# A hybrid decoder layer on one core: the GLU takes its columns by position in the chunk, and the last block's early u is computed from unscaled x

## The chip, the cores and the metric

The kernel runs on one core of one Trainium2 chip, as one program. The metric is the device time of one execution in microseconds (us). The engines are named as in the profile: PE is TensorE's matmul, PEld its weight load, DVE is VectorE, ACT is ScalarE, POOL is GpSimd, and SP is SyncE, which here issues most of the DMAs.

## The reference, cut to what matters

One decoder layer over 2064 tokens (16 meta tokens and 2048 others) of 1024 features, all in fp32:

```python
hn = rms_norm(h, norm_mix_g)                 # h * rsqrt(mean(h*h) + eps) * g
proj = hn @ w_in                             # columns: b_gate | c_gate | v | u, 512 each
conv_out = b_gate * causal_dwconv(c_gate * v, conv_w)       # width 3
y = s5(u)                                    # 32 groups, complex diagonal state, scan over tokens
g = gelu(y)
ssm_out = g * sigmoid(g @ w_glu)             # the GLU, 512 x 512
mixed = concat(rms_norm(conv_out), rms_norm(ssm_out))
h = h + mixed @ w_out
hn = rms_norm(h, norm_ffn_g)
up = causal_dwconv(hn @ w_up, ffn_conv_w, ffn_conv_b)       # 2 x 2816 columns
h = h + (silu(up[:2816]) * up[2816:]) @ w_down
y = rms_norm(h, norm_final_g)                # meta positions dropped
```

The 1/rms of a token is one number for all its features. So `proj` of a token can be computed from `x * g` without it, and be multiplied by it afterwards: `(x * g * rs) @ w = rs * ((x * g) @ w)`.

## The kernel before, in words

Features lie on the 128 partitions, tokens along the free dimension. The 2064 tokens are cut into six chunks of 344 columns (`QL`), numbered 0 to 5 (q), and three blocks of two chunks each (b = 0, 1, 2; 688 columns, `B2`). A chunk of x is loaded in two halves of four k-tiles (128 x 4 x 344, 688 KB).

**Every matmul is made of three.** Both operands are split into a high part (rounded to the matmul's fp32r format, a copy on ScalarE) and a low part (what is left, a subtraction on VectorE): `split_weights` (L122) for weights, `parts` (L246) for activations, which is the pair L248 and L109 in the profile. `product` (L128) issues high x high (L138), high weights x low activations (L139) and low weights x high activations (L142) for each k-tile, into one PSUM tile for both chunks of a block. With `by_chunk` all of chunk 0 comes first, then all of chunk 1; otherwise the chunks alternate by k-tile. Three PSUM tiles (`mm_tile`, L95) are in rotation.

**1/rms.** `inv_rms` (L173) squares the halves on ScalarE (L164, two buffers of tag `sq`), adds them on VectorE to one row of 344 columns (L109), sums over the partitions by matmuls with a column of ones (`st_...`, L188), takes the power -1/2 on GpSimd (L199), spreads the result on diagonals (`dg_...`, L203), broadcasts it to all partitions by a matmul (`sb_...`, L208), and copies it from PSUM on ScalarE (`rs_...`, L213).

**x in, two ways.** `raw_x` (L378) is used for chunks 0 and 1, at the kernel's start: it splits `x * g` at once, four k-tiles of a half by four short instructions on ScalarE (L389) and four on VectorE (L390), and computes 1/rms beside it, into the tile `rs0`; the products of block 0 are multiplied by it when they leave PSUM. `prep_x` (L348) is used for all others: it loads, computes 1/rms, scales x by g and 1/rms into a new tile (`t_c`, L241, eight short VectorE instructions for a chunk; tag `sq`), and splits that (L248, L109, one long instruction each for a half). With `late` the split is put off and emitted where `take_late` stands. The halves of x have three buffers (tag `xt`).

**Order of the work.** First u of block 0 (`u_block(0)`), then `conv_block(0)`, then u of block 2 (the "early u"), u of block 1, `conv_block(1)`, `conv_block(2)`. Beside block 0 the coefficients of the state space are computed, in memory (pool `a0`) that is given free when they are done; `start_a1` then opens the pools `xf2` (four split tiles) and `a1` in its place. There `prep_x(4, hu, other=True)` and `prep_x(5, hu, late=late)` are queued, chunks 4 and 5 for the early u: chunk 4's split goes to `xf2`, chunk 5's to the tiles that chunk 0 leaves after the last unit of `conv_block(0)`. The scan itself runs beside `conv_block(1)` and `conv_block(2)`. In the text the side work is made of generators, stepped after each unit; the framework then orders each engine's instructions with the text's order as priority and a model of durations, and inserts the waits. So an instruction can stand earlier on its engine than in the text, and an engine keeps the order that was set even where the chip's times are others.

`u_block` (L877) writes u from PSUM to `ut` in order of position in the chunk: token 8c + j goes to row j, column c. It does so on VectorE for block 0, where 1/rms is multiplied in (`mul`, L890), and on ScalarE otherwise (L892). The state space works on u in this order, and its result after gelu lies in DRAM (`g_d`) the same way.

**The GLU.** `load_glu` (L1012) brings the result into `gt`, 128 x 4 x 8 x 258: feature group, position j, column c. The matmuls want two-dimensional chunks of 344 columns. `tokens` (L1007) is a view of such a chunk that reads or writes it in the order of j, then c, with neighbours eight columns apart, so that the chunk itself is in token order. `prep_glu` (L1016) splits each chunk of `gt` through this view (`gh` on ScalarE, L1021; `gl` on VectorE, L109). `glu_block` (L1072) has four units of 24 matmuls for each chunk pair (`pg`), takes the sigmoid (`sg`, L1079) and multiplies `gt` by it in place, again through `tokens` (L1081). `prep_ssm` (L1026) norms and splits the result for the output projection, in token order (L1038, and `l_ms`, L1039), as x and the other half of the projection are in token order.

The tile for 1/rms of a whole block has one buffer (`rs_tile`, L373, tag `rsk`); after the projection it serves the MLP's norms (`prep_rs`, L1108). The MLP, from about 700 us to the end, is not touched.

Of the kernel before, what the change touches and what calls it, by code (L numbers as in the profile page):

```python
# [14 lines left out]
AF = mybir.ActivationFunctionType  # L15
ALU = mybir.AluOpType
# [6 lines left out]
NJ = 8  # L23
# [5 lines left out]
QL = 344  # L29
# [28 lines left out]
def layer_kernel(ctx, tc, xq, pk, w_in, w_glu, w_out, w_up, w_down, ssm_s, ssm_m, y):  # L58
    nc = tc.nc
    V, S, T, G = nc.vector, nc.scalar, nc.tensor, nc.gpsimd  # L60
# [7 lines left out]
    xf2 = None  # L68
# [33 lines left out]
    def f32(ap):  # L102
        return ap.bitcast(F32)

    def two(ap):
        return ap.rearrange("p (c t) -> p c t", c=2)

    def tt(out, a, b, op):
        V.tensor_tensor(out, a, b, op=op)  # L109

    def mul(out, a, b):
        tt(out, a, b, ALU.mult)
# [37 lines left out]
    def hl_tile(n, name, pool=None, tag="xhl", bufs=8):  # L150
        return (pool or xf).tile([P, 4, QM], F32R, tag=tag, bufs=bufs, name=name)[:, :, :n]
# [21 lines left out]
    def inv_rms(groups, n, name, out=None):  # L173


        s = sum_squares(groups, n, name)
        yield
        yield
        return (yield from inv_rms_of(s, 4 * P * len(groups), n, name, out))
# [193 lines left out]
    def rs_tile(name):  # L373
        return cp.tile([P, 2, QM], F32, tag="rsk", bufs=1, name=name)

    rs0 = rs_tile("rs0")[:, :, :QL]

    def raw_x(q, res):  # L378


        xs, out = [], []
        for i in range(2):
            xs += load_halves((xq[q, :, 4 * i : 4 * i + 4, :],), QL, f"c{q}{i}")
            yield
        for i, x in enumerate(xs):
            hi, lo = hl_tile(QL, f"h_c{q}_{i}"), hl_tile(QL, f"l_c{q}_{i}")
            for k in range(4):
                g = col(C_MIX + 4 * i + k)
                S.activation(hi[:, k, :], x[:, k, :], AF.Copy, scale=g)  # L389
                V.scalar_tensor_tensor(  # L390
                    out=lo[:, k, :], in0=x[:, k, :], scalar=g, in1=f32(hi[:, k, :]), op0=ALU.mult, op1=ALU.subtract
                )
            out.append((hi, lo))
            yield
        res.append(out)
        yield from inv_rms(xs, QL, f"c{q}", rs0[:, q, :])


    sgn = col(C_SGN)
# [456 lines left out]
    def after_unit(n=1, n_prep=1):  # L856
        if a1 is None:
            ssm.step(4)
            if not ssm.q:
                start_a1()  # L860
                prep.add(prep_x(4, hu, other=True), prep_x(5, hu, late=late))
        else:
            ssm.step(n)
            prep.step(n_prep)
# [12 lines left out]
    def u_block(b, hs, last=False):  # L877
        rhs = rhs_of(hs)
        for m in range(4):
            if last and m == 3:  # L880
                while len(late) < 2:
                    prep.step()
            ps = unit(rhs, f"pu_{b}_{m}", m == 0 or last and m == 3)
            ut = cvp.tile([P, NJ, 86], F32, tag="ut", bufs=2, name=f"ut_{b}_{m}")
            if last and m == 3:
                take_late(2)
            by_j = lambda a: a.rearrange("p c (x j) -> p c x j", j=NJ)
            out = ut.rearrange("p j (c x) -> p c x j", c=2)
            if b == 0:
                mul(out, by_j(ps[:, :, :QL]), by_j(rs0))  # L890
            else:
                S.activation(out, by_j(ps[:, :, :QL]), AF.Copy)  # L892
            dma(out=u_d[:, m, :, b * 86 : b * 86 + 86].rearrange("j p c -> p j c"), in_=ut)
            after_unit(n_prep=5 if last else 1)

    def conv_block(b, hs, late_after=False, n_prep=1):
        rhs = rhs_of(hs)

        for j in range(4):
            pv_ = unit(rhs, f"cv_{b}_{j}", False)  # L900
            vs = cvp.tile([P, B2], F32, tag="cs", bufs=3, name=f"vs_{b}_{j}")
            if b == 0:
                mul(two(vs), pv_[:, :, :QL], rs0)
            else:
                S.activation(two(vs), pv_[:, :, :QL], AF.Copy)
            after_unit(n_prep=n_prep)
            pc = unit(rhs, f"cc_{b}_{j}", False)
            cv = cvp.tile([P, B2 + 2], F32, tag="cvt", bufs=1, name=f"cvt_{b}_{j}")
            V.tensor_copy(cv[:, 0:2], halo[:, j, :])
            if b == 0:  # L910
                mul(two(vs), two(vs), rs0)
            tt(two(cv[:, 2:]), pc[:, :, :QL], two(vs), ALU.mult)
            V.tensor_copy(halo[:, j, :], cv[:, B2 : B2 + 2])
            tp = cvp.tile([P, B2], F32, tag="cs", bufs=3, name=f"tc_{b}_{j}")
            S.activation(tp, cv[:, 2:], AF.Copy, scale=col(C_CW + 8 + j))
            axpy(tp, cv[:, 1 : B2 + 1], col(C_CW + 4 + j), tp)
            axpy(tp, cv[:, 0:B2], col(C_CW + j), tp)
            if b == 0:
                mul(two(tp), two(tp), rs0)
            after_unit(n_prep=n_prep)  # L920
            if late_after and j == 3:
                while len(late) < 2:
                    prep.step()
            pb = unit(rhs, f"cb_{b}_{j}", j == 3)
            if late_after and j == 3:
                take_late(2)
            tt(two(tp), pb[:, :, :QL], two(tp), ALU.mult)
            dma(out=mx_d[2 * b : 2 * b + 2, :, j, :].rearrange("q p t -> p q t"), in_=two(tp))
            after_unit(n_prep=n_prep)
# [37 lines left out]

    hc = [[] for _ in range(3)]
    hu, late = [], []
    first = [raw_x(q, hc[0]) for q in range(2)]  # L970
    next(first[0])
    stream.raw.append(load_weights(*stream.items.popleft()))
    next(first[0])
# [5 lines left out]
    while first:  # L979
        for g in list(first):  # L980
            if next(g, prep) is prep:
                first.remove(g)
    u_block(0, hc[0])
    conv_block(0, hc[0], late_after=True, n_prep=4)

    prep.add(prep_x(2, hc[1]), prep_x(3, hc[1], other=True, late=late))
# [20 lines left out]
    def tokens(a):  # L1007

        names = "p k (c j) -> p k j c" if len(a.shape) == 3 else "p (c j) -> p j c"
        return a.rearrange(names, j=NJ)  # L1010
# [5 lines left out]
    def prep_glu(b, res, **kw):  # L1016
        for c in range(2):
            hi, lo = hl_tile(QL, f"gh_{b}_{c}", **kw), hl_tile(QL, f"gl_{b}_{c}", **kw)
            c0 = (2 * b + c) * 43
            src = gt[:, :, :, c0 : c0 + 43]  # L1020
            S.activation(tokens(hi), src, AF.Copy)  # L1021
            tt(tokens(lo), src, f32(tokens(hi)), ALU.subtract)
            res.append(((hi, lo),))
            yield

# [46 lines left out]
    def glu_block(b):  # L1072
        until(hg[b])
        rhs = rhs_of(hg[b])
        for m in range(4):
            ps = mm_tile(f"pg_{b}_{m}")
            product([ps[:, c, :QL] for c in range(2)], stream.take(), rhs, 4, by_chunk=m == 0)
            sg = ev_tile(f"sg_{b}_{m}")
            S.activation(two(sg), ps[:, :, :QL], AF.Sigmoid)  # L1079
            g = gt[:, m, :, b * 86 : b * 86 + 86]  # L1080
            mul(g, g, tokens(sg))  # L1081
            prep.step(2 if b else 1)

    hos = [[] for _ in range(3)]
# [587 lines left out]
```

## Time and profile before

| | |
|---|---|
| time, median of 3 runs | 2195.66 us (2195.51 to 2199.68) |
| the profiled execution's own time | 2199.4 us |
| its span, first to last instruction | 2197.6 us |
| granted TensorE clock, mean | 0.984 |
| busy DVE, share of the span | 77% |
| busy ACT, share of the span | 50% |

The profile is one execution. Each row of a group or of the order in time names the line, engine, operation, and `out<-in` by the program's tile names; durations are us unless marked ns; `[1.79 <-DVE sq_ms L109]` means that the engine stood idle for 1.79 us until VectorE finished writing `sq_ms`. A weight load (PEld) overlaps matmuls. The granted clock of a stretch is the mean share of TensorE's full clock. DMA-issuing instructions on SP show the time of the issue, not of the transfer.

### The profile page before, as it was taken

How to read it: one execution, taken by the hardware profiler on the slowest of the kernel's cores; microseconds unless marked ns; L12 is line 12 of the kernel's file. 1: busy time of each engine (PE TensorE's matmuls, PEld its weight loads, DVE VectorE, ACT ScalarE, POOL GpSimd, SP SyncE). 2: the span in 40 equal slices, each digit the busy share in tenths (PEclk: the TensorE clock that was granted, in tenths of full speed). 3: DMA queues.
4: the chain of work that ended last, by engine and by line, in shares of the span. 5: the costliest groups of instructions: out<-in, count | busy, mean ns of one | idle time of the engine just before them, and what ended most of it. 6: DMA issues, size and time to landing. Idle time of an engine off the chain costs nothing.

```text
span 2197.6 us, 33162 instructions
## 1 busy us (share of the span) xinstructions
PE 2119.1 (96%) x13012; PEld 2057.7 (94%) x13012; DVE 1688.0 (77%) x2539; ACT 1097.5 (50%) x1651; POOL 153.2 (7%) x174
## 2 busy tenths in 40 slices
PE   8997999999899999999999999999999999999997
PEld 7997999998898999999999999999899999999996
DVE  8896498857866796886679878777768878767776
ACT  4135333236523365554556556555456556545555
POOL 0000000000000001101110010100111010110010
PEclk9998999999999999999999999999999999999999
DMA  7376544352475336635552554744554362654463
GB/s 246 104 219 169 142 144 146 116 169 74 144 232 187 100 98 158 157 90 122 133 127 76 144 119 122 184 103 130 147 136 109 103 166 82 163 118 99 98 168 118
DMA packets 170750, 300.29 MB, mean 137 GB/s; under 512 B 32416, under 2 KB 104800, under 8 KB 170464
## 3 DMA queue, kind: packets, MB, share of 16 engines
q1 hardware_dynamic: 149856, 246.41, 36.3%
q0 software_dynamic: 19584, 47.52, 13.0%
q10 hardware_dynamic: 1152, 4.23, 0.5%
q8 instruction: 102, 1.67, 0.3%
q14 instruction: 56, 0.46, 0.1%
HBM read 214.29 MB, written 83.82 MB: 136 GB/s over the span
## 4 chain that ended last, share of the span: by engine, by line
PE 60%; issue 8%; DVE 5%; ACT 3%; DMA 3%; POOL 1%; SPq 0%; POOLq 0%; DVEq 0%; ACTq 0%
PE xy L1427 9%; PE xy L1429 8%; PE xy L1428 8%; PE dn L138 6%; PE dn L139 6%; PE dn L142 6%; PE pz L1429 3%; PE pz L1427 3%; PE pz L1428 3%; PE po L138 2%; PE po L142 2%; PE po L139 1%; DMA v_b<-h_d 1%; DMA gt<-g_d 1%; ACT h_ms L1038 1%
## 5 line engine op out<-in xcount | busy, mean ns | idle before, releaser
L109 DVE TENSOR_TENSOR wl_up<-wr_up,wh_up 128x1024 fp32r<-128x1024 f32 x198 | 241.8, 1222 | 140.7 <-ACT wh_up L248 138.5
L138 PE MATMUL dn<-ah,wh_dn 128*128 128x344 f32 (+1 forms) x1024 | 327.8, 324 | 11.4 <-ACT ah L248 8.8
L139 PE MATMUL dn<-al,wh_dn 128*128 128x344 f32 (+1 forms) x1024 | 325.5, 321 | 0.4 <-DVE al L109 0.3
L248 ACT ACTIVATE wh_up<-wr_up 128x1024 fp32r<-128x1024 f32 x198 | 209.6, 1059 | 230.8 <-PE dn L139 56.4
L1427 PE MATMUL xy<-h_t,wh_up 128*128 128x344 f32 (+1 forms) x792 | 262.8, 332 | 0.0
L1429 PE MATMUL xy<-h_t,wl_up 128*128 128x344 f32 (+1 forms) x792 | 253.4, 320 | 0.0
L1428 PE MATMUL xy<-l_t,wh_up 128*128 128x344 f32 (+1 forms) x792 | 252.7, 319 | 0.0
L142 PE MATMUL dn<-ah,wl_dn 128*128 128x344 f32 (+1 forms) x1024 | 248.1, 321 | 0.0
L138 PEld LDWEIGHTS dn<-ah,wh_dn 128*128 128x128 f32 x1024 | 193.2, 189 | 17.1 <-ACT ah L248 9.7
L1529 POOL DMA_DIRECT2D h_d<-ev x136 | 118.3, 870 | 1261.8 <-ACT ev L1525 1251.4
L139 PEld LDWEIGHTS dn<-al,wh_dn 128*128 128x128 f32 x1024 | 194.2, 190 | 2.0 <-DVE al L109 1.2
L1427 PE MATMUL xy<-h_b,wh_up 128*128 128x344 f32 (+1 forms) x528 | 175.6, 334 | 6.1 <-ACT ev L1525 4.6
L142 PEld LDWEIGHTS dn<-ah,wl_dn 128*128 128x128 f32 x1024 | 178.4, 190 | 0.0
L1428 PE MATMUL xy<-l_b,wh_up 128*128 128x344 f32 (+1 forms) x528 | 169.0, 320 | 0.0
L1429 PE MATMUL xy<-h_b,wl_up 128*128 128x344 f32 (+1 forms) x528 | 167.6, 320 | 0.0
L1427 PEld LDWEIGHTS xy<-h_t,wh_up 128*128 128x128 f32 x792 | 149.2, 188 | 17.1 <-ACT z L1472 11.1
L248 ACT ACTIVATE wh_dn<-wr_dn 128x512 fp32r<-128x512 f32 (+1 forms) x144 | 85.5, 594 | 133.6 <-issue 56.7
L1428 PEld LDWEIGHTS xy<-l_t,wh_up 128*128 128x128 f32 x792 | 149.9, 189 | 0.0
L1429 PEld LDWEIGHTS xy<-h_t,wl_up 128*128 128x128 f32 x792 | 149.6, 189 | 0.0
L115 DVE SCALAR_TENSOR_TENSOR g<-z,pv,g 128x688 f32<-128x688 f32 (+1 forms) x132 | 122.3, 926 | 23.7 <-ACT g L1432 22.9
L115 DVE SCALAR_TENSOR_TENSOR v<-z,pneg,v 128x688 f32<-128x688 f32 (+1 forms) x132 | 122.4, 927 | 10.3 <-ACT v L1432 9.0
L109 DVE TENSOR_TENSOR wl_dn<-wr_dn,wh_dn 128x512 fp32r<-128x512 f32 (+1 forms) x144 | 92.3, 644 | 45.6 <-ACT wh_dn L248 44.9
(413 smaller groups left out, 5358.3 us busy)
## 6 DMA issues: line engine op xcount, KB each, us to landing
wr_up<-in_w_up SPq DMA_DIRECT2D x132, 512.0 KB, 5.0
h_d<-ev POOLq DMA_DIRECT2D x88, 344.0 KB, 6.6
wr_dn<-in_w_down SPq DMA_DIRECT2D x96, 256.0 KB, 2.6
wr_cw<-in_w_in SPq DMA_DIRECT2D x36, 512.0 KB, 4.6
h_d<-ev POOLq DMA_DIRECT2D x48, 336.0 KB, 6.7
x_c<-in_xq SPq DMA_DIRECT2D x16, 688.0 KB, 6.4
wr_dn<-in_w_down SPq DMA_DIRECT2D x48, 192.0 KB, 2.3
xr<-in_xq SPq DMA_DIRECT2D x24, 344.0 KB, 3.7
```

Of the source, the lines that this page charges most:

```text
L109: V.tensor_tensor(out, a, b, op=op)
L115: V.scalar_tensor_tensor(out=out, in0=a, scalar=s, in1=b, op0=ALU.mult, op1=ALU.add)
L138: T.matmul(ps[c], hi[:, k, :], xh, start=k == 0, stop=False)
L139: T.matmul(ps[c], hi[:, k, :], xl, start=False, stop=False)
L142: T.matmul(ps[c], lo[:, k, :], xh, start=False, stop=k == nk - 1)
L248: S.activation(hi, t, AF.Copy)
L1038: S.activation(tokens(hi), t, AF.Copy)
L1427: T.matmul(ps, hi[:, j, :], xh[:, j, :], start=start and j == 0, stop=False, **kw)
L1428: T.matmul(ps, hi[:, j, :], xl[:, j, :], start=False, stop=False, **kw)
L1429: T.matmul(ps, lo[:, j, :], xh[:, j, :], start=False, stop=j == 3, **kw)
L1529: G.dma_start(out=h_d[:, m, s0 : s0 + no], in_=ev, accum_op=ALU.add)
```

## The change

Two things are changed.

In the GLU, `gh` and `gl` now keep the order of `gt` within a chunk, j then c: the chunk's 344 columns are eight runs of 43, both where they are read and where they are written. The sigmoid comes out in this order too, and the product views `gt` as (chunk, j, column), so that both sides run in order.

For the early u, chunks 4 and 5 go through `raw_x` in place of `prep_x`: `x * g` is split without 1/rms, in short instructions; 1/rms goes to a block tile `rs_of[2]` in the buffer that `rs_of[0]` had; and u of block 2 is multiplied by it on VectorE when it leaves PSUM. The loads of chunk 4 are emitted ahead of `conv_block(0)`; the split of chunk 4 still goes to `xf2`, the split of chunk 5 is still put off by `late`. Conv of block 2 still uses `prep_x`, which loads chunks 4 and 5 once more.

```diff
-    rs0 = rs_tile("rs0")[:, :, :QL]
-    def raw_x(q, res):
+    rs_of = {}
+    def raw_x(q, res, b, other=False, late=None):
         xs, out = [], []
+        kw = dict(pool=xf2, tag="xhl2", bufs=4) if other else {}
         for i in range(2):
             xs += load_halves((xq[q, :, 4 * i : 4 * i + 4, :],), QL, f"c{q}{i}")
             yield
-        for i, x in enumerate(xs):
-            hi, lo = hl_tile(QL, f"h_c{q}_{i}"), hl_tile(QL, f"l_c{q}_{i}")
+        if other:
+            kw["pool"] = xf2
+        def split_half(i, x):
+            hi, lo = hl_tile(QL, f"h_c{q}_{i}", **kw), hl_tile(QL, f"l_c{q}_{i}", **kw)
             for k in range(4):
...
             out.append((hi, lo))
+            if i == 1:
+                res.append(out)
+        for i, x in enumerate(xs):
+            if late is None:
+                split_half(i, x)
+            else:
+                late.append(lambda x=x, i=i: split_half(i, x))
             yield
-        res.append(out)
-        yield from inv_rms(xs, QL, f"c{q}", rs0[:, q, :])
+        if b not in rs_of:
+            rs_of[b] = rs_tile(f"rs_{b}")[:, :, :QL]
+        yield from inv_rms(xs, QL, f"c{q}", rs_of[b][:, q % 2, :])
...
                 start_a1()
-                prep.add(prep_x(4, hu, other=True), prep_x(5, hu, late=late))
+                prep.add(ahead[0], raw_x(5, hu, 2, late=late))
...
-            if b == 0:
-                mul(out, by_j(ps[:, :, :QL]), by_j(rs0))
+            if b in rs_of:
+                mul(out, by_j(ps[:, :, :QL]), by_j(rs_of[b]))
             else:
                 S.activation(out, by_j(ps[:, :, :QL]), AF.Copy)
...
     u_block(0, hc[0])
+    ahead = [raw_x(4, hu, 2, other=True)]
+    next(ahead[0])
+    next(ahead[0])
     conv_block(0, hc[0], late_after=True, n_prep=4)
...
             src = gt[:, :, :, c0 : c0 + 43]
-            S.activation(tokens(hi), src, AF.Copy)
-            tt(tokens(lo), src, f32(tokens(hi)), ALU.subtract)
+            hj, lj = (a.rearrange("p k (j c) -> p k j c", j=NJ) for a in (hi, lo))
+            S.activation(hj, src, AF.Copy)
+            tt(lj, src, f32(hj), ALU.subtract)
...
             S.activation(two(sg), ps[:, :, :QL], AF.Sigmoid)
-            g = gt[:, m, :, b * 86 : b * 86 + 86]
-            mul(g, g, tokens(sg))
+            g = gt[:, m, :, b * 86 : b * 86 + 86].rearrange("p j (c x) -> p c j x", c=2)
+            mul(g, g, two(sg).rearrange("p c (j x) -> p c j x", j=NJ))
```

The other uses of `rs0` become `rs_of[0]`, and the first two chunks are made by `raw_x(q, hc[0], 0)`.

More of the change, by code (lines that the diff above doesn't have):

```diff
@@ L902, in conv_block @@
             if b == 0:
-                mul(two(vs), pv_[:, :, :QL], rs0)
+                mul(two(vs), pv_[:, :, :QL], rs_of[0])
             else:
@@ L910, in conv_block @@
             if b == 0:
-                mul(two(vs), two(vs), rs0)
+                mul(two(vs), two(vs), rs_of[0])
             tt(two(cv[:, 2:]), pc[:, :, :QL], two(vs), ALU.mult)
@@ L918, in conv_block @@
             if b == 0:
-                mul(two(tp), two(tp), rs0)
+                mul(two(tp), two(tp), rs_of[0])
             after_unit(n_prep=n_prep)
@@ L969, in layer_kernel @@
     hu, late = [], []
-    first = [raw_x(q, hc[0]) for q in range(2)]
+    first = [raw_x(q, hc[0], 0) for q in range(2)]
     next(first[0])
```

## The prediction

> **What bounds the kernel now.** I read the page first, then the table of stretches, then the order of time on TensorE around the stretches that fall short, and last the groups of instructions there.
>
> ```profile
> span 2197.6 us, 33162 instructions
> ...
> PE 2119.1 (96%) x13012; PEld 2057.7 (94%) x13012; DVE 1688.0 (77%) x2539; ACT 1097.5 (50%) x1651; POOL 153.2 (7%) x174
> ```
>
> TensorE is the bound: busy 96% of the span. An edit to VectorE or ScalarE work pays only where TensorE stands for it, or runs at a lower clock after standing. The stretches (columns: bounds, length, then busy us and count of PE, PEld, DVE, ACT, POOL, granted clock, DMA share, GB/s) show where:
>
> ```profile
> 140.00:160.00 20.00, 20.00 (x128) 20.00 (x127) 18.07 (x25) 8.76 (x9) 0.00 (x0) 1.00 0.92 274
> 160.00:180.00 20.00, 8.90 (x35) 7.07 (x34) 15.54 (x25) 6.56 (x6) 1.20 (x1) 0.66 0.70 218
> ...
> 200.00:220.00 20.00, 16.47 (x101) 15.18 (x100) 13.15 (x20) 11.41 (x11) 0.85 (x1) 1.00 0.73 187
> ...
> 500.00:520.00 20.00, 17.74 (x104) 17.46 (x102) 18.64 (x10) 19.97 (x16) 0.00 (x0) 0.91 0.17 53
> 520.00:540.00 20.00, 17.95 (x101) 17.52 (x101) 17.72 (x24) 10.26 (x14) 2.03 (x2) 0.87 0.29 80
> 540.00:560.00 20.00, 18.57 (x109) 17.43 (x107) 16.07 (x21) 11.75 (x12) 1.17 (x1) 0.96 0.05 14
> 560.00:580.00 20.00, 15.96 (x88) 15.79 (x89) 17.34 (x27) 8.81 (x13) 1.17 (x1) 0.83 0.45 141
> ```
>
> A full slice holds 128 matmuls, 20/128 = 0.156 us each. 160:180 is the early u of the last block: 93 are missing, 14.5 us. 200:220 is where u of block 1 begins: 27 missing, 4.2 us. The GLU, 500:580, misses 24+27+19+40 = 110, 17.2 us. The change touches the first and the third, and moves work that feeds the second.
>
> In the first stretch, in order of time on TensorE:
>
> ```profile
> 161.16 0.32 PE L139 MATMUL pu<-l_c,wh_u 128*128 128x344 f32 x1
> 164.82 0.76 PE L188 MATMUL st_c<-ones,sq_c 128*115 128x1 f32 x6 [3.33 <-DVE sq_c L109]
> 168.50 1.52 PE L208 MATMUL sb_c<-dg_c,ones 115*128 115x344 f32 x2 [2.92 <-DVE dg_c L203]
> 174.02 1.23 PE L138 MATMUL pu<-h_c,wh_u 128*128 128x344 f32 x3 [4.00 <-ACT h_c L248]
> ```
>
> Chunk 4 of x is there, chunk 5 isn't: TensorE waits for its squares (3.33), for its diagonal (2.92), then for the high parts (4.00), a chain from 1/rms to the split. In the GLU, ScalarE, TensorE and VectorE:
>
> ```profile
> 497.62 2.90 ACT L1021 ACTIVATE gh<-gt 128x1376 fp32r<-128x1376 f32 x1 [3.34 <-DMA gt<-g_d]
> 500.29 0.81 ACT L1064 ACTIVATE kp<-pk 128x688 f32<-128x688 f32 x1
> ...
> 504.77 0.32 PE L138 MATMUL pg<-gh,wh_g 128*128 128x344 f32 x1
> ...
> 506.76 0.69 DVE L109 TENSOR_TENSOR wl_g<-wr_g,wh_g 128x512 fp32r<-128x512 f32 x1
> ...
> 507.51 0.65 PE L142 MATMUL pg<-gh,wl_g 128*128 128x344 f32 x1 [2.26 <-DVE wl_g L109]
> ...
> 524.87 0.73 ACT L1079 ACTIVATE sg<-pg 128x688 f32<-128x688 f32 x1
> ...
> 534.60 1.20 PE L188 MATMUL st_ms<-ones,sq_ms 128*115 128x1 f32 x6 [1.79 <-DVE sq_ms L109]
> ...
> 564.04 1.29 PE L188 MATMUL st_mc<-ones,sq_mc 128*115 128x1 f32 x6 [4.87 <-DVE sq_mc L109]
> ```
>
> All three stalls end on VectorE, which is behind: 18.64, 17.72, 16.07 and 17.34 of 20 us busy.
>
> **The GLU, part by part.** The groups from 480 to 620 us (count, busy us, mean ns):
>
> ```profile
> L109 DVE TENSOR_TENSOR gt<-gt,sg 128x688 f32<-128x688 f32 x12 | 17.8, 1486 | 2.7 <-ACT sg L1079 2.7
> L1021 ACT ACTIVATE gh<-gt 128x1376 fp32r<-128x1376 f32 x6 | 17.6, 2938 | 3.3 <-DMA gt<-g_d 3.3
> L109 DVE TENSOR_TENSOR gl<-gt,gh 128x1376 fp32r<-128x1376 f32 x6 | 17.5, 2914 | 10.6 <-ACT gh L1021 10.5
> ...
> L109 DVE TENSOR_TENSOR l_ms<-t_ms,h_ms 128x1376 fp32r<-128x1376 f32 x4 | 12.1, 3018 | 1.9 <-ACT h_ms L1038 1.7
> ...
> L109 DVE TENSOR_TENSOR xr<-po,xr 128x688 f32<-128x688 f32 x9 | 7.8, 867 | 0.5 <-PE po L142 0.5
> ...
> L164 ACT ACTIVATE sq_ms<-gt 128x1376 f32<-128x1376 f32 x4 | 5.4, 1365 | 4.7 <-DVE gt L109 3.5 <-DVE l_mc L109 1.2
> ...
> L109 DVE TENSOR_TENSOR l_mc<-t_mc,h_mc 128x1376 fp32r<-128x1376 f32 x2 | 3.2, 1586 | 0.0
> ...
> L248 ACT ACTIVATE h_mc<-t_mc 128x1376 fp32r<-128x1376 f32 x2 | 2.7, 1356 | 2.2 <-DVE t_mc L241 2.2
> ```
>
> gh, gl and the product with sg step over columns eight apart; the change takes them in order, in runs of 43. sq_ms reads the same runs of gt in 1.37 us, the time of h_mc with long rows, so runs cost nothing there. I price gh at 1.36 (h_mc), gl at 1.59 (l_mc), the product at 0.87 (xr<-po). ScalarE saves 6 x 1.58 = 9.5 us, VectorE 6 x 1.33 + 12 x 0.62 = 15.4 us. l_ms, which keeps its columns, stays at 3.0.
>
> First stall: gt lands at 497.62. gh ends at 499.0, gl at 500.6; the second gh, behind one kp eviction (0.8), at 501.2, its gl at 502.8, wl_g (0.69) at 503.5, before the 504.77 at which TensorE wants it. Block 0 is a third of the GLU's matmuls, 4 x 24 = 96, so 15.0 us: from 504.77 it ends at 519.8, not at the 524.87 of its last sigmoid: **5.0**. Second stall: from 519.8, sigmoid 0.73, product 0.87, two squares 1.37 each, sums of 688 and 344 columns about 1.4 (0.87 and half of it): 525.5, and the 48 matmuls before st_ms end at 527.3. The stall (1.79) goes, and what followed it: clocks of 0.87 and 0.96 are 5.2 + 1.6 = 6.8 us if reckoned as half clock (the matmul at 507.51 takes 0.65, the one at 504.77 0.32), 3.4 us of work: **5.2**. Third stall: VectorE has two l_ms of 3.0 in front, which stay; three products lie in that chain (the last two of block 1, the first of block 2), 3 x 0.62 = 1.9 off 4.87; I take **1.5** and leave its slow clock. Sum 11.7. Nothing is added, and no wait moves to SP or POOL.
>
> Of the first stall's 5.0, 2.26 is standing and some 1.8 the clock (0.91 is 3.6 us at half speed). The Trainium skill, "TensorE: Matmul & The Clock Gate" (Part 1), has the clock halve after an idle window of about 3.4 us. The trace has it halved after 2.26 and 1.79, so the measurement decides. By that rule 1.8 and 3.4 would not be won, and the sum would be 6.5; this is my lower bound for the part, by rows the case that another wait keeps the clock low. Upper bound: the third stall goes too, 3.4 more and 3.4 of clock, 18.5.
>
> **The early u of the last block.** Rows for its parts (groups; the first split of the kernel, in time; SP's loads in time; DMA landing for x between 130 and 230 us, and for line 661):
>
> ```profile
> L109 DVE TENSOR_TENSOR l_c<-t_c,h_c 128x1376 fp32r<-128x1376 f32 x8 | 12.4, 1590 | 0.0
> ...
> L892 ACT ACTIVATE ut<-pu 128x688 f32<-128x688 f32 x6 | 9.0, 1497 | 0.0
> ...
> L109 DVE TENSOR_TENSOR ut<-pu,rs 128x688 f32<-128x688 f32 x4 | 6.0, 1493 | 0.0
> ```
> ```profile
> 6.76 2.00 ACT L389 ACTIVATE h_c<-x_c,pv 128x344 fp32r<-128x344 f32 x4
> 7.38 2.04 DVE L390 SCALAR_TENSOR_TENSOR l_c<-x_c,pv,h_c 128x344 fp32r<-128x344 f32 x4 [5.90 <-ACT h_c L389]
> ...
> 34.24 0.43 SPq L258 DMA_DIRECT2D x_c<-in_xq  x1
> ...
> 147.86 1.23 SPq L258 DMA_DIRECT2D x_c<-in_xq  x1
> ...
> DMA to landing us min/median/max: 4.2/5.8/8.0
> ```
> ```profile
> L661 SPq DMA_DIRECT2D mat_d<-vm x2: 359/818/1277, 139.5 to 143.6; - x2
> ...
> DMA to landing us min/median/max: 5.1/6.2/7.2
> ...
> 153.78 0.87 DVE L109 TENSOR_TENSOR tc<-tc,rs 128x688 f32<-128x688 f32 x1
> ```
>
> Removed: four l_c of 1.59 on VectorE (6.4 us) and the wait of chunk 5's split for its 1/rms; scaling and subtraction become the sixteen short ones that were t_c. Moved: four evictions of u from ScalarE (1.50) to VectorE (1.49, the row of u's block 0), 6.0 us over four units; VectorE leaves 4.5 and 6.9 us idle in 160:180 and 200:220, which hides them, and without that cover they cost the 6.0. The loads issued ahead gain and cost nothing on SP: x_c goes out at 34.24 already and then not until 147.86, since three buffers hold what is loaded. So the second half of chunk 5 is the last to come.
>
> Added: (a) that load now waits until chunk 4's first half is split, not scaled. The split writes memory that the matrices (vm, issued last at 143.6, landing by at most 7.2: 150.8) have held. Split from 151.2 to 153.7 (2.0, and 0.5 behind), load 5.8 (4.2 to 8.0): 159.5 (157.9 to 161.7), high parts 2.0, low parts 0.5 more: 162.0 (to 164.2). TensorE wants chunk 5 at 161.2 and its second half 12 matmuls, 1.9 us, later: 163.1. (b) VectorE, busy 18.07 of 20 us just before, gets eight more short splits (4 us) there. Standing left is 0 to 1.1 by (a) and 0 to 4 by (b); I take 2.2, and 1.8 of clock as behind the GLU's first stall: 4.0, with bounds 0 and 8. (c) rs of block 2 shares one buffer with rs of block 0, read last at 153.78: ScalarE writes it after 154.7; behind that write can stand chunk 5's high parts, up to 3.4 us, inside the 8. (d) The eviction of u now waits for both 1/rms: squares, sums and broadcast follow the landing by some 14 us (the old ones: landed by 156, broadcast done at 170.0), about 174. Three PSUM tiles let TensorE run until 161.2 + 3.8 + 15.0 = 180, so it is covered.
>
> 14.5 less 0.5 for the eight small matmuls that stay, less 4.0: **10.0** (6 to 14).
>
> Next late: block 1. Its chunks' loads, squares and scalings follow chunk 5's buffers, and TensorE comes for them about 10 us sooner. Those buffers come free sooner as well, as no t_c of chunk 5 holds one until 174. I take the 4.2 of 200:220 as unchanged: 0 (a gain of 4 to a loss of 4).
>
> **Sum.** 11.7 + 10.0 = 21.7 off the profiled execution's 2199.4 (span 2197.6 and 1.8 around it): 2177.7. That execution lay 3.7 above the median of the runs, 2195.66, so **2174**. Ends: 6.5 + 6 - 4 = 8.5 gives 2187; 11.7 + 3 (part of the third stall) + 14 + 4 = 32.7 gives 2163.
>
> **Rivals.** *Given back at block 1*: the chain to chunk 3 ends when it did, and TensorE waits at 190 for what it won at 161. For it: three x buffers and two for squares are handed on in turn, and the slice 200:220 is short by 4.2 already. Against it: the hand-on starts sooner. GLU alone: 2195.7 - 11.7 = 2184, with another slow clock 2187. *Strides cost VectorE nothing*: gl and the product stay at 2.91 and 1.49, only ScalarE is quicker; wl_g comes at about 505.6 and VectorE stays behind, perhaps 4 of 11.7 are won: 2182. Against it stands l_ms at 3018 beside l_mc at 1586, the same operation and shape. The Trainium skill, "VectorE: DVE Perf Modes" (Mode 1×), says just this: fp32 with two tensors runs one element a cycle, "weird strides" included; the trace disagrees by 1.9 times. *More*: the third stall and block 1's waits go too: 2158 to 2166. *Not what it says*: chunk 5's 1/rms still stands ahead of its matmuls in TensorE's order, so the new load time (153.7 against 147.9) eats the first gain, and the products slow down in runs of 43: 2192 to 2200. *Slower*: the eviction of u waits at VectorE's head for 1/rms, and behind it stand wl_u for TensorE and block 1's sums; every us that 1/rms comes after 180 costs one, and from 180 + 21.7 + 4 = 206 on the kernel is slower: for 1/rms at 210, about 2204. Against it: that is 32 us later than (d) has it.
>
> **Chances.** Forecast 0.60 (2168 to 2183), given back 0.17, strides 0.04, more 0.09, not what it says 0.06, slower 0.04. A measurement of this kernel tells some 0.2%, 4.4 us, from no change. Faster 0.90, same 0.06, slower 0.04. The range, 2163 to 2187, leaves out the last two, most of "more", and some edges.
>
> **What would show it.** Right: gl near 1.6 us and gh near 1.36, the product near 0.87; no stall before pg's first wl_g, none at st_ms; 160:180 with over 100 matmuls; u of block 2 evicted on VectorE. Wrong: gl still near 2.9; a wait of over 8 us at 161 for h_c or st_c; a wait at u of block 1 larger than the 4.2 us now.

## The result, and the profile after

The changed kernel takes 2178.89 us (median of 4 runs, 2176.4 to 2182.5), the kernel before beside it 2195.59 us (median of 4, 2193.84 to 2199.68). The ratio is 0.9923, with a 95% interval of 0.9903 to 0.9942: 17 us faster, 13 to 21. The forecast was 2174, range 2163 to 2187. The profiled execution after took 2178.72 us, 20.7 below that of before; the prediction's sum for it was 2177.7.

The head of the page of the changed kernel:

```profile
span 2177.0 us, 33169 instructions
...
PE 2112.7 (97%) x13012; PEld 2053.0 (94%) x13012; DVE 1671.2 (77%) x2539; ACT 1089.1 (50%) x1659; POOL 153.6 (7%) x174
```

The stretches of the changed kernel; the last is everything behind the output projection, to the end:

```profile
160.00:180.00 20.00, 19.34 (x124) 18.57 (x123) 18.83 (x29) 10.03 (x13) 1.37 (x2) 1.00 0.91 278
180.00:200.00 20.00, 18.57 (x116) 17.80 (x115) 18.47 (x26) 7.93 (x7) 1.32 (x1) 1.00 0.88 202
200.00:220.00 20.00, 13.09 (x58) 11.59 (x58) 12.04 (x18) 8.40 (x7) 0.85 (x1) 0.66 0.41 110
500.00:520.00 20.00, 20.00 (x129) 20.00 (x128) 13.63 (x15) 13.64 (x19) 0.00 (x0) 1.00 0.39 106
520.00:540.00 20.00, 20.00 (x129) 19.17 (x127) 16.21 (x34) 12.32 (x16) 2.95 (x3) 1.00 0.14 41
540.00:560.00 20.00, 15.67 (x84) 15.21 (x83) 15.60 (x21) 9.59 (x12) 1.17 (x1) 0.83 0.28 91
...
728.40:2177.00 1448.60, 1419.39 (x8805) 1379.27 (x8804) 1114.24 (x1502) 811.89 (x1330) 128.67 (x146) 0.99 0.49 125
```

The same two stretches of the kernel before that the prediction did not show:

```profile
180.00:200.00 20.00, 20.00 (x128) 19.62 (x127) 13.22 (x20) 10.57 (x10) 0.85 (x1) 1.00 0.61 131
...
745.80:2197.60 1451.80, 1420.54 (x8805) 1380.70 (x8804) 1114.47 (x1502) 809.79 (x1330) 128.67 (x146) 0.99 0.49 125
```

The early u's hole is filled: 124 matmuls in 160:180 for 35, which is 89 x 0.156 = 13.9 us. A new hole stands in 200:220: 58 matmuls for 101, at a clock of 0.66. From 160 to 220 us the kernel before ran 35 + 128 + 101 = 264 matmuls, the changed one 298: 5.3 us are left of the 13.9. The first two GLU stretches are full at a clock of 1.00; the third has the third stall and its slow clock. Behind the output projection nothing was changed, and yet 3.2 us went there (1451.8 to 1448.6). That need not come from the change: over the twelve kernels profiled here that leave this stretch as it is, it takes 1445.3 to 1452.8 us.

By stages, from first matmul to first matmul of the next: conv of block 0 ends 2.3 us later, u of blocks 2 and 1 together ("both u" below) are 5.6 us shorter (84.0 to 78.3), the GLU 10.4 (67.7 to 57.3), the output projection 3.7, the rest 3.2. Together that is the 20.6 us by which the span is shorter.

The groups of the GLU's stage in the changed kernel (480 to 620 us):

```profile
L109 DVE TENSOR_TENSOR l_ms<-t_ms,h_ms 128x1376 fp32r<-128x1376 f32 x4 | 12.1, 3032 | 2.6 <-ACT h_ms L1055 2.4
...
L109 DVE TENSOR_TENSOR gt<-gt,sg 128x688 f32<-128x688 f32 x12 | 10.5, 878 | 4.6 <-ACT sg L1096 4.6
...
L109 DVE TENSOR_TENSOR gl<-gt,gh 128x1376 fp32r<-128x1376 f32 x6 | 9.5, 1588 | 8.6 <-ACT gh L1038 8.6
...
L1038 ACT ACTIVATE gh<-gt 128x1376 fp32r<-128x1376 f32 x6 | 8.3, 1376 | 3.4 <-DMA gt<-g_d 3.4
```

The three prices are those forecast: gl 1.59, gh 1.38, the product 0.88.

And where TensorE still stands, in order of time on TensorE:

```profile
199.28 0.76 PE L188 MATMUL st_c<-ones,sq_c 128*115 128x1 f32 x6 [1.15 <-DVE sq_c L109]
202.11 1.51 PE L208 MATMUL sb_c<-dg_c,ones 115*128 115x344 f32 x2 [2.07 <-DVE dg_c L203]
207.63 1.23 PE L138 MATMUL pu<-h_c,wh_u 128*128 128x344 f32 x3 [4.01 <-ACT h_c L248]
209.70 0.65 PE L139 MATMUL pu<-l_c,wh_u 128*128 128x344 f32 x1 [0.84 <-DVE l_c L109]
...
549.89 1.29 PE L188 MATMUL st_mc<-ones,sq_mc 128*115 128x1 f32 x6 [4.33 <-DVE sq_mc L109]
```

The four waits that chunk 5 caused before are back, almost line for line, at chunk 3: sum of squares, diagonal, high parts, low parts, 8.1 us. Before, 189 matmuls of u lay ahead of these sums; now it is 220, and 220 is all that the order of work has ahead of chunk 3's split, in both kernels: 192 of u of block 2, the 24 of block 1's first unit with chunk 2, and four more of the units behind it.

Why is chunk 3 not sooner? VectorE's last sums of squares of chunks 2 and 3, in the kernel before (the second row holds two instructions):

```profile
183.73 0.51 DVE L109 TENSOR_TENSOR sq_c<-sq_c 128x344 f32<-128x344 f32 x1
...
203.83 1.43 DVE L109 TENSOR_TENSOR sq_c<-sq_c 128x688 f32<-128x688 f32 x2
```

and in the changed kernel, with what lies between them on VectorE, ScalarE and SP's queue:

```profile
177.69 0.53 DVE L109 TENSOR_TENSOR sq_c<-sq_c 128x344 f32<-128x344 f32 x1
...
178.12 1.39 DVE L109 TENSOR_TENSOR ut<-pu,rs 128x688 f32<-128x688 f32 x1
...
186.66 2.33 SPq L258 DMA_DIRECT2D x_c<-in_xq  x2
...
188.50 3.11 DVE L109 TENSOR_TENSOR l_c<-t_c,h_c 128x1376 fp32r<-128x1376 f32 x2
...
190.12 1.36 ACT L164 ACTIVATE sq_c<-x_c 128x1376 f32<-128x1376 f32 x1
...
191.52 1.54 DVE L109 TENSOR_TENSOR ut<-pu,rs 128x688 f32<-128x688 f32 x1
191.64 1.37 ACT L164 ACTIVATE sq_c<-x_c 128x1376 f32<-128x1376 f32 x1 [0.16 <-DVE l_c L109]
...
195.53 1.44 DVE L109 TENSOR_TENSOR ut<-pu,rs 128x688 f32<-128x688 f32 x1
...
198.73 0.50 DVE L109 TENSOR_TENSOR sq_c<-sq_c 128x344 f32<-128x344 f32 x1
```

From chunk 2's sums to chunk 3's it is 21.0 us in both kernels (184.2 to 205.3; 178.2 to 199.2). The steps are the same; that their sum is the same is in part chance, as from the sums to the copy of 1/rms it was 7.7 us before and is 5.9 now, and from there to chunk 3's sums 13.3 and 15.1. The whole chain came 6.0 us sooner. TensorE came 14.5 us sooner: the last of the 220 matmuls started at 212.4 and starts now at 197.8. The difference, 8.5 us, is lost again there, in waits and in the slow clock behind them. Two theories for the length of the chain: **H1**, the evictions that moved to VectorE (ut rows) stand among the sums; **H2**, buffers are handed on: chunk 3's squares write the two buffers in which chunk 2's scaled x lies until it is split (190.1 and 191.6, when the two l_c end), and its second half is loaded only at 186.66, when chunk 2's first half has been scaled.

### The profile page after: what moved, and what is told of

The parts are those of the page before. It is cut to its first block, busy times and chain, and to the rows that moved or that the text cites. A ratio compares the mean times of both kernels' runs of the same rounds, so it can differ in the third digit from the quotient of the medians.

```text
span 2177.0 us, 33169 instructions
## 1 busy us (share of the span) xinstructions
PE 2112.7 (97%) x13012; PEld 2053.0 (94%) x13012; DVE 1671.2 (77%) x2539; ACT 1089.1 (50%) x1659; POOL 153.6 (7%) x174
## 5 line engine op out<-in xcount | busy, mean ns | idle before, releaser
L138 PE MATMUL dn<-ah,wh_dn 128*128 128x344 f32 (+1 forms) x1024 | 327.7, 324 | 10.2 <-ACT ah L248 8.9
L1444 PEld LDWEIGHTS xy<-h_t,wh_up 128*128 128x128 f32 x792 | 148.9, 188 | 18.3 <-ACT z L1489 11.4
L1446 PEld LDWEIGHTS xy<-h_t,wl_up 128*128 128x128 f32 x792 | 149.3, 188 | 0.0
```

What stands on the lines that cost most here:

```text
L138: T.matmul(ps[c], hi[:, k, :], xh, start=k == 0, stop=False)
L1444: T.matmul(ps, hi[:, j, :], xh[:, j, :], start=start and j == 0, stop=False, **kw)
L1446: T.matmul(ps, lo[:, j, :], xh[:, j, :], start=False, stop=j == 3, **kw)
```

## The experiments

All ratios are to the kernel before, run on the same chip, with 95% intervals. The changed kernel itself is 0.9923.

**1. The GLU's part alone**: the kernel before with the last two pieces of the diff.

> The kernel before with the GLU's part of the change alone. Main theory (the two parts add up; the GLU carries most): the first two stalls of the GLU go, the time from the first matmul of pg to the last falls from 67.7 us to 57 to 58, the half-clock window at 606 goes too, and the time is 11 to 14 us below the kernel before, about 2183. Rival (the GLU won only beside the earlier part, and the clock windows moved by chance): a gain under 7 us.

Measured 0.9945 (0.9932 to 0.9959): 12 us, 9 to 15. The GLU takes 57.1 us. The half clock at 606 us is gone, but that tells nothing: it is gone without the GLU's part too (experiment 2). In the kernel before it followed a wait of 1.83 us for `xr` in the output projection. Ten of the other kernels profiled here have this wait at 1.8 to 1.9 us, three of them with a half clock behind it and seven without.

**2. The early u's part alone**: the changed kernel with those two pieces undone.

> The changed kernel with the GLU's part undone, so the early u's part alone. Main theory (given back at block 1's u, and 2.3 us lost in conv of block 0): the early u has no stall over 1 us, but block 1's u stands for about 8 us and conv of block 0 ends 2.3 us late; net 3 to 4 us faster than the kernel before, about 2192. Rival (the full price of the prediction, 10 us): about 2186. Other rival (nothing left): within 1 us of the kernel before.

Measured 0.9972 (0.9962 to 0.9982): 6 us, 4 to 8. 160:180 has 124 matmuls, 200:220 has 63 at a clock of 0.74. 12.1 and 6.2 add up to 18.3, and the whole change gave 17: within the intervals the parts add up, and about two thirds of it is the GLU.

**3. Without the loads ahead.**

```diff
-                prep.add(ahead[0], raw_x(5, hu, 2, late=late))
+                prep.add(raw_x(4, hu, 2, other=True), raw_x(5, hu, 2, late=late))
```

> The changed kernel without the loads ahead of conv of block 0: chunk 4 is queued where chunk 5 is, as in the kernel before. Main theory (the loads' early place in the text also gives chunk 4's first sum of squares an early place on VectorE, in its full stretch at 36 us, and this costs 2.3 us): conv of block 0 ends at about 157 us again and the time is about 2 us below the changed kernel. Rival (the loads ahead help the early u): chunk 4 and 5 come later, the early u stands for 2 us or more, and the time is the same or above the changed kernel's.

In the changed kernel chunk 4's first sum of squares stands at 36 us on VectorE, in the midst of the coefficient work and ahead of the eviction of u:

```profile
36.15 1.59 DVE L109 TENSOR_TENSOR sq_c<-sq_c,sq_c 128x1376 f32<-128x1376 f32 x1
37.66 1.44 DVE L109 TENSOR_TENSOR ut<-pu,rs 128x688 f32<-128x688 f32 x1
```

and `kps`, which waits for the coefficients, comes 1.5 us later than in the kernel before, where it stood at 83.93:

```profile
85.47 0.73 PE L616 MATMUL kps<-w,mats 128*128 128x16 f32 x5 [1.04 <-DVE w L611]
```

Without the loads ahead it is back:

```profile
84.17 1.06 PE L616 MATMUL kps<-w,mats 128*128 128x16 f32 x8 [1.01 <-DVE w L611]
```

But the time is not: 0.9920 (0.9905 to 0.9934). TensorE waits 1.7 us in all for `tq` at 110 to 117 us, where the changed kernel waits 1.3 and the kernel before 0.6. Neither theory's difference was there, and the early u did not stand without the loads ahead either. Most of the 2.3 us has another source: among the eight kernels here with the changed kernel's start and three buffers for x, four have the clock halved for 13.65 us from about 88 us on, and need 149.3 to 149.6 us from the start of the first u matmul to that of the early u's first; four have it halved for 10.24 us, and need 147.6 to 148.0. With the start of the kernel before it is 149.0 in the one case (one kernel) and 147.1 to 147.2 in the other (two). The stretch 80:105 of the changed kernel, and of the kernel of experiment 4, which is the same up to there:

```profile
80.00:105.00 25.00, 23.96 (x133) 23.47 (x133) 14.37 (x28) 3.99 (x7) 0.00 (x0) 0.73 0.36 113
```
```profile
80.00:105.00 25.00, 23.94 (x143) 23.49 (x143) 15.36 (x34) 4.20 (x7) 0.00 (x0) 0.80 0.38 122
```

So the changed start costs 0.3 to 0.9 us, and not by the loads ahead: without them it is 148.7, with the clock halved for 10.24 us (one kernel). The other 1.7 is one step of the clock more or less (3.41 us at half clock), which falls out differently where the order of work up to there is the same.

**4. The eviction later in the text**, behind the five steps of preparation of its unit.

> The changed kernel with block 2's eviction of u emitted after the five steps of preparation of its unit, so that it stands behind the sums of squares of chunks 2 and 3 on VectorE and not in front. Theory H1 (the four evictions that moved to VectorE stand in the chain to chunks 2 and 3 and so make block 1's u wait): the stalls in 198 to 211 us fall from 8.0 us to about 3 to 5, and with the slow clock behind them the time falls by 4 to 8 us against the changed kernel. Theory H2 (the chain is set by the hand-on of the x buffers and their loads): the stalls stay at 7 to 9 us and the time within 2 us of the changed kernel.

Measured 0.9919 (0.9904 to 0.9933), with the same four waits (1.13, 2.07, 4.01, 0.84). It tells nothing between H1 and H2: VectorE's order came out the same, ut in front of the sums, since the order follows modelled times and not the text alone. It serves as a repetition of the changed kernel.

**5. The eviction without its multiplication**, on ScalarE again.

```diff
-            if b in rs_of:
+            if b == 0:
```

> The changed kernel with block 2's u evicted on ScalarE by a copy, as in the kernel before; its multiplication by 1/rms is left out, so u of block 2 is not normed. Tells whether the four evictions on VectorE make block 1's u wait. Theory H1 (they stand among chunk 2's and chunk 3's sums of squares, about 2.9 + 2.2 us): chunk 3's sums come about 5 us sooner against block 2's u, the stalls at block 1's u fall from 8.0 us to about 3, and the time falls by 4 to 8 us against the changed kernel, to a ratio of 0.989 to 0.990. Theory H2 (the hand-on of the buffers for x and for the squares sets the chain): the stalls stay at 7 to 9 us, the ratio at 0.992.

On TensorE:

```profile
198.08 0.73 PE L188 MATMUL st_c<-ones,sq_c 128*115 128x1 f32 x6 [0.58 <-DVE sq_c L109]
...
200.89 1.37 PE L208 MATMUL sb_c<-dg_c,ones 115*128 115x344 f32 x2 [1.17 <-DVE dg_c L203]
206.27 1.23 PE L138 MATMUL pu<-h_c,wh_u 128*128 128x344 f32 x3 [4.01 <-ACT h_c L248]
208.34 0.66 PE L139 MATMUL pu<-l_c,wh_u 128*128 128x344 f32 x1 [0.84 <-DVE l_c L109]
```

The waits fall from 8.1 to 6.6 us, not to 3; chunk 3's sums end at 197.9 in place of 199.2. The ratio is 0.9908 (0.9894 to 0.9921), 3 us below the changed kernel's, and the intervals overlap. From chunk 2's sums to chunk 3's it is 19.5 us in place of 21.0. H1 has a share of 1.5 us in the chain and in the waits, and no more.

**6. The multiplication on GpSimd**, in place, after ScalarE's copy.

```diff
+            if b == 2:
+                G.tensor_tensor(out, out, by_j(rs_of[b]), op=ALU.mult)
```

> The changed kernel with block 2's u copied out of PSUM on ScalarE and multiplied by 1/rms in place on GpSimd, so all of the computation is there. H1: as without the scaling, stalls of about 3 us and a ratio of 0.989 to 0.990, less what GpSimd's work costs VectorE. H2: stalls of 7 to 9 us, 0.992. If GpSimd's work hinders VectorE: stalls of 8 us or more.

Measured 0.9947 (0.9934 to 0.9959), 5 us above the changed kernel. GpSimd's rows, then VectorE's at that time:

```profile
174.44 2.75 POOL L907 TENSOR_TENSOR ut<-ut,rs 128x688 f32<-128x688 f32 x1 [4.49 <-ACT rs L213]
177.48 2.29 POOL L907 TENSOR_TENSOR ut<-ut,rs 128x688 f32<-128x688 f32 x1 [0.28 <-ACT ut L905]
```
```profile
175.20 2.72 DVE L109 TENSOR_TENSOR sq_c<-sq_c 128x688 f32<-128x688 f32 x1
177.84 2.49 DVE L109 TENSOR_TENSOR ct<-wr,wi 128x544 f32<-128x544 f32 x1
```

VectorE's add, of 0.87 us elsewhere, starts at 175.20 and ends 0.7 us after GpSimd's first multiplication (177.2); the next, of 0.72 elsewhere, ends 0.6 after the second (179.8). VectorE waited out each of them, and in the end TensorE stood 4.2 us for chunk 2's sums and 3.8 for chunk 3's. Of the two places tried with the multiplication in, VectorE is the better.

**7. A fourth buffer for x, chunks 2 and 3 side by side** (memory from three other tiles).

```diff
-    def half_tile(n, name, tag="xt", bufs=3):
+    def half_tile(n, name, tag="xt", bufs=4):
...
+    prep.lanes = 2
     prep.add(prep_x(2, hc[1]), prep_x(3, hc[1], other=True, late=late))
```

> The changed kernel with a fourth buffer for x, and chunks 2 and 3 prepared side by side, so that chunk 3's squares need no longer wait for chunk 2's scaling and split; the memory comes from three other tiles' second or third buffers, which slows other stages, so only the stalls at block 1's u count. Theory H2 (the hand-on of buffers sets the chain from chunk 2 to chunk 3): chunk 3's sums end by 190 us in place of 199 and the stalls at block 1's u fall from 8.0 us to 2 or less. H1 (VectorE's load): chunk 3's sums come 3 us sooner at most, with 5 us or more of standing.

VectorE's sums of chunks 2 and 3, and TensorE's one wait of over 0.3 us after 185 us:

```profile
173.60 0.50 DVE L109 TENSOR_TENSOR sq_c<-sq_c 128x344 f32<-128x344 f32 x1
...
180.91 0.50 DVE L109 TENSOR_TENSOR sq_c<-sq_c 128x344 f32<-128x344 f32 x1
```
```profile
202.47 0.42 PE L139 MATMUL pu<-l_c,wh_u 128*128 128x344 f32 x1 [0.72 <-DVE l_c L109]
```

H2 holds against H1. The sums end at 174.1 and 181.4, 7.3 us apart in place of 21.0, with all four evictions still on VectorE, and both u together take 66.2 us in place of 78.3. The fourth buffer also let chunk 5's 1/rms go ahead of the early u, and two things were changed at once (the buffer, and the order that uses it; the squares keep their two buffers), so the run does not price them apart. The kernel as a whole takes 2200.8 us in its one run. The GLU is not what makes it slow (57.7 us); the output projection is, at 196.2 us in place of 169.5. There the tiles `xr` are down to one buffer of three, and TensorE stands for them, longest here:

```profile
577.52 0.63 PE L138 MATMUL po<-h_ms,wh_o 128*128 128x344 f32 x1 [7.04 <-DVE xr L109]
```

**8. TensorE's order at block 1's u**: the three PSUM tiles take the products of three units with chunk 2 first.

```diff
+        for i in range(group):
+            w = stream.take() if i < 2 else stream.ready.popleft()
+            ps = mm_tile(f"pu_{b}_{i}")
+            product([ps[:, 0, :QL]], w, lambda k, _: rhs(k, 0), KD)
+            head.append((w, ps))
...
-    u_block(1, hc[1])
+    u_block(1, hc[1], group=3)
```

> The changed kernel with TensorE's order at block 1's u changed: the products of the first three units with chunk 2 come first (72 matmuls in place of 24), then those with chunk 3. Theory (what block 1's u gives back is TensorE arriving at chunk 3 before its split; 48 matmuls, 7.5 us, cover it): the stalls there fall from 8.0 us to 1 or 2, most of the slow clock behind them goes, and the time falls by 6 to 11 us against the changed kernel, to a ratio of 0.987 to 0.9895. Rival (the chain to chunk 3 itself waits for TensorE, by the evictions of u or the weights): it moves out with TensorE's order, and the ratio stays at 0.991 to 0.993.

The stretch, and the waits there:

```profile
200.00:220.00 20.00, 18.89 (x117) 18.14 (x116) 13.02 (x18) 11.92 (x11) 0.15 (x1) 1.00 0.48 138
```
```profile
198.20 0.76 PE L188 MATMUL st_c<-ones,sq_c 128*115 128x1 f32 x6 [0.67 <-DVE sq_c L109]
...
201.03 0.85 PE L208 MATMUL sb_c<-dg_c,ones 115*128 115x344 f32 x2 [0.70 <-DVE dg_c L203]
...
207.95 0.43 PE L139 MATMUL pu<-l_c,wh_u 128*128 128x344 f32 x1 [0.41 <-DVE l_c L109]
```

Measured 0.9887 (0.9871 to 0.9903): 2171.19 us, some 8 us below the changed kernel (2 to 13). The chain to chunk 3 is not shorter (21.0 us); it is covered. The waits are 1.8 us, the clock stays at 1.00, both u take 68.6 us.

**9. The same order without the early u's part** (GLU's part and new order only).

> The kernel before with the GLU's part and with TensorE's order at block 1's u changed (three units with chunk 2 first), without the early u's part. It prices the early u's part where block 1's u cannot take it back. If the prediction's step is right and only its cover was missing, this kernel is 10 us or more above the one with both parts and the same order (0.9887): 0.993 to 0.995, no better than the GLU alone (0.9945) by more than 2 us, with the early u standing for about 11 us as before. Rival (the new order is what gains, the early u's part is worth 5 us at most): 0.989 to 0.991.

Measured 0.9937 (0.9923 to 0.9950), no better than the GLU alone within the intervals; 160:180 has 39 matmuls again. Against experiment 8 the early u's part is worth 0.0050, 11 us (6 to 16), where it was worth 6 without the cover. By itself the new order gains some 2 us over the GLU alone, which is not clear of noise; its worth is that it lets the early u keep its own.

**10. The product back on strides**, the splits in runs (the sigmoid writes in token order).

> The changed kernel with the GLU's product back on columns eight apart: the sigmoid writes in token order, and the product reads it with a stride, as before; the splits stay in runs. By the prediction's terms the product is 1.49 us again in place of 0.87, 12 x 0.62 = 7.4 us of VectorE. Theory (the splits carry the first stall, the product part of the second and third): the time from pg's first matmul to its last is 58 to 61 us in place of 57.3, the time 1 to 4 us above the changed kernel. Rival (the products carry half of it): 62 to 64 us, 5 us or more above the changed kernel.

The groups of this kernel:

```profile
L1096 ACT ACTIVATE sg<-pg 128x688 f32<-128x688 f32 x12 | 17.9, 1495 | 7.0 <-PE pg L142 7.0
L109 DVE TENSOR_TENSOR gt<-gt,sg 128x688 f32<-128x688 f32 x12 | 17.9, 1488 | 6.7 <-ACT sg L1096 6.7
```

The GLU takes 61.5 us, 4.2 of its 10.4 are lost, and the ratio is 0.9948 (0.9936 to 0.9961), 5 us above the changed kernel. The GLU's time lies between the two forecasts, and it is an upper bound for the product, as the sigmoid doubled too (0.74 to 1.50 us).

**11. The last split of the stage in runs too**, on top of experiment 8: the four short scalings write t_ms in token order.

```diff
-                out=t[:, k], in0=src[:, k]
+                out=tokens(t)[:, k], in0=src[:, k]
...
-        S.activation(tokens(hi), t, AF.Copy)
-        tt(tokens(lo), t, f32(tokens(hi)), ALU.subtract)
+        parts(t, hi, lo)
```

> The changed kernel with the new order at block 1's u, and the last split of the GLU's stage in runs as well: the four short scalings write t_ms in token order, eight columns apart, so that h_ms and l_ms go over long rows. Theory (a stride costs VectorE wherever it stands): the scalings go from 0.57 to about 1 us each, l_ms from 3.0 to 1.6, h_ms from 2.9 to 1.4; VectorE is even, ScalarE gains 1.5 us for each of six, and the time stays within 3 us of the kernel with the new order alone (0.9887). Rival (a strided write alone costs nothing): the scalings stay at 0.57, VectorE gains 1.4 us for each, the third stall shrinks by 2 us or more, and the time falls by 2 to 5 us.

```profile
L1062 DVE SCALAR_TENSOR_TENSOR t_ms<-gt,pv,rs_ms 128x344 f32<-128x344 f32 x16 | 12.3, 886 | 0.0
...
L109 DVE TENSOR_TENSOR l_ms<-t_ms,h_ms 128x1376 fp32r<-128x1376 f32 x4 | 6.4, 1596 | 0.0
...
L248 ACT ACTIVATE h_ms<-t_ms 128x1376 fp32r<-128x1376 f32 x4 | 5.4, 1360 | 4.7 <-DVE t_ms L1062 4.7
```
```profile
537.33 0.73 PE L188 MATMUL st_mc<-ones,sq_mc 128*115 128x1 f32 x6 [1.35 <-DVE sq_mc L109]
```

Neither forecast: a strided write makes a scaling 0.89 us in place of 0.57, less than expected, so four cost 1.3 us more where l_ms gains 1.4 and h_ms 1.6. VectorE's work is even, as the theory had it; what gains is that h_ms is done sooner, for which l_ms waited (2.6 us idle ahead of the four l_ms in the changed kernel, none here). The third stall falls from 4.4 us in experiment 8 to 1.35, the slow clock behind it goes, and the ratio is 0.9852 (0.9832 to 0.9872): 2164.34 us, some 8 us below experiment 8 (2 to 13) and the fastest kernel of the study.

## Why the prediction was right or wrong

The direction, the range and the mechanism of both parts held. One step failed, block 1; a surplus of the early u made up for part of it.

- **GLU, 11.7 forecast.** Alone it gave 12 us (experiment 1), in the profile 10.4. The prices were right, the first two stalls went, and with them 10.2 us of slow clock (windows at 507 and 534), worth 5.1. The lower bound of 6.5 wasn't needed. (It came from the Trainium skill, "TensorE: Matmul & The Clock Gate" (Part 1), with its idle window of about 3.4 us; the slow clock that went with stalls of 2.26 and 1.79 us disagrees.) Too high was the third stall, 1.5 forecast, 0.5 measured (4.87 to 4.33): it hangs mostly on the strided h_ms and l_ms, as experiment 11 shows, and by 1.2 us at most on the products (5.54 in experiment 10, where the sigmoid is slower too).
- **VectorE pays for strides.** The rival by which strides cost it nothing is out: gl fell from 2.91 to 1.59 us as only its columns changed. (The Trainium skill, "VectorE: DVE Perf Modes" (Mode 1×), has one result a cycle in this mode and says that "weird strides" work in it; it gives no price for them, and the trace has 1.8 times for gl.)
- **Early u, 10.0 forecast.** The hole itself gave 13.9 us, the upper end: the 4.0 for standing and slow clock wasn't needed, TensorE stands 0.9 us in all from 160 to 185 us. Chunk 5's second half did come late, issued at 158.3 and landed at 162.4 against 159.5 (157.9 to 161.7) in (a), but TensorE came 2.3 us late too. That lateness of conv of block 0 the prediction had not: some 1.7 of it is the clock, 0.3 to 0.9 the changed start (experiment 3). Where block 1 is covered, the part is worth 11 us (experiment 9).
- **Block 1, 0 forecast with bounds of 4: this step failed.** 200:220 lost 43 matmuls, 6.7 us, 180:200 twelve more, 1.9. The prediction said that the buffers "come free sooner as well, as no t_c of chunk 5 holds one until 174". They did, by 6 us; but what follows is a chain, 21 us from chunk 2's sums to chunk 3's through buffers that chunk 2 still holds, and TensorE comes 14.5 us sooner: 8.5 are lost. It should have been laid out as a chain with its length, and TensorE's arrival set beside it. The rival "given back at block 1" (0.17) was the true course for 8.6 of the 13.9 us, and it named the cause, the buffers for x and for squares handed on in turn. Early u and block 1 together, 10.0 forecast, gave 6 us (4 to 8, experiment 2).
- **The four evictions on VectorE, whose idle time "hides them".** Nearly: they cost 1.5 us of the waits at block 1 (experiment 5).
- **Loads ahead, "gain and cost nothing on SP".** True of the time within what can be measured (0.9920 without, 0.9923 with). But a side effect on another engine was overlooked, an early sum of squares on VectorE, which delays `kps` by 1.3 us (experiment 3).
- **The evictions' wait for 1/rms (d), "covered".** True: the first comes at 174.5, and TensorE does not stand for it.
- **The sum.** 21.7 forecast, 20.7 in the profiles, 16.7 by the medians. That the profiles come so near to the forecast is luck, as 6.9 of the 20.7 were in no term. The output projection gave 3.7: a halved clock of 3.41 us at 606 us went, 1.7 us of work, and some 2.0 us of waits, most of them for sums of squares. The clock is no effect of the change that these runs show, as it comes and goes behind the same wait (experiment 1). The 3.2 behind the output projection lie in unchanged work, within what it varies by; without them, the terms come to 17.5, near the medians.

## What to carry to other kernels

When a stall ahead of a unit is removed, lay out the chain that feeds the next unit as a length in us, from the event that starts it to the buffer that ends it, and set it against TensorE's new arrival: what moves up less than TensorE is given back, however free the engines are. Such a chain need not be shortened: with PSUM tiles to spare, work that doesn't need its end can go first (experiment 8). And of several strided passes over the same data put the stride where it adds least: here 0.3 us to each of four short scalings, 1.3 in all, against 1.4 and 1.6 us to the two long passes behind them.

## What the runs showed of the hardware

- **A stride of eight fp32 columns**, by what is strided: VectorE, one of two operands read with it (the product) 1486 ns for 878; the output alone written with it (t_ms) 886 for 573; an operand and the output (gl) 2914 for 1588. ScalarE, output alone, 2938 for 1376 (gh) and 1495 for 738 (the sigmoid). Runs of 43 columns cost nothing on either. The Trainium skill, "SBUF — State Buffer" (Door 1: The DMA port swizzle), has lines of 16 bytes, four fp32, and a penalty for each access to a new line, without its size; the rows agree in kind, as each of these accesses is 32 bytes from the last.
- **GpSimd's multiplication of two tensors stops VectorE's two-tensor work** until it ends: of the four VectorE instructions that started during one in experiment 6, 0.87 became 2.72 and 2.65 us, 0.72 became 2.49, a weight's low part of 1.22 became 2.77, and each ended 0.6 to 1.1 us behind it. One that already ran when GpSimd's began kept its time (an l_c of 1.58 us). The Trainium skill, "SBUF — State Buffer" (SBUF: two separate sides), calls the port pair that both share an exclusive lock for the whole instruction when VectorE reads two tensors; these rows agree.
- **The clock is halved after short waits too, and not always**: in the kernel before at 507.4 us, within a wait of 2.26 us, and at 534.7, just behind one of 1.79; in the changed kernel from 200.6 us on, in the second of two waits of 1.15 and 2.07 us. But the wait of 1.8 us for `xr` in the output projection halved it in four kernels and left it whole in seven. It stays halved for 3.41 us or a multiple of it (6.83, 10.24, 13.65, 17.07) in all traces here, but for the stretch that the kernel's end cuts off. So a short stall can cost more by what follows it than by itself: the 1.79 us were followed by 6.83 us at half clock, which is 3.4 us of work.
